# A decoder layer with 32 experts on one core: weights in rows of 8 KB, two tiles for the halves' sums, and later one-hot rows at the last expert

## The chip, the core and the metric

The kernel runs on one core of a Trainium2 chip. The core has TensorE (PE, whose weight loads the profile shows as PEld), VectorE (DVE), ScalarE (ACT), GpSimd (POOL), SyncE (SP, which here issues nearly all transfers) and 16 DMA engines. The metric is the time of one execution on the device in microseconds; less is better.

## What is computed

A decoder layer for 256 tokens of width 1024, all in float32: a projection, two kinds of attention, an output projection, a LayerNorm, and then a mixture of 32 experts of which each token uses four. The experts' part is what the change is about. Cut to that:

```
def moe_ffn(h, w_router, b_router, w1, b1, w2, b2):
    logits = (h @ w_router + b_router)
    top_vals, top_idx = lax.top_k(logits, 4)
    gates = jax.nn.softmax(top_vals, axis=-1)
    ...
    def expert_block(xb, e):                  # tokens of expert e
        act = clamped_swiglu(xb @ w1[e] + b1[e])   # w1[e]: 1024 x 2048, w2[e]: 1024 x 1024
        return act @ w2[e] + b2[e]
    ...
    # every token: sum of its four experts' rows, weighted by gates

def clamped_swiglu(h):
    glu = jnp.minimum(h[..., 0::2], 7.0)
    lin = jnp.clip(h[..., 1::2], -7.0, 7.0)
    return glu * jax.nn.sigmoid(1.702 * glu) * (lin + 1.0)
```

All 32 experts are evaluated, so all weights, 32 x 12.6 MB, pass through the core once.

## The kernel before, in words

The attention comes first (to about 146 us), then a Python loop unrolls the experts e = 0 to 31.

**Weights.** An expert has twelve blocks of 1 MB. Eight are of `w1`: a block holds 256 rows by one half of the columns, so that a partition gets two pieces of 4 KB; blocks 0 to 3 are the first half (n = 0), 4 to 7 the second. Four are of `w2`: 256 whole rows, a partition gets row p and row p + 128, again two pieces of 4 KB. The list `stream` has all 384 blocks in the order in which they are wanted, but for the last four, which are `w2` of the last expert cut by columns, in pieces of 2 KB. There are 23 places of 8 KB a partition (`place`; fifteen in the tile `arena`, eight tiles `later`), and block i goes into the place of block i - 23. `load(n)` writes the transfers up to block n into SP's program; SP works in order, and each transfer waits until the block that had its place has been read. Where they are written: for the experts 0 to 3, 30 and 31 (those that are not `inline`) behind every second step of the first product; for the others in one go, twelve behind the first step of the next expert, since a branch for experts with more than 64 tokens (`more`, taken if the count of expert e - 1 asks for it) stands there and reads the blocks again.

**One expert.** Up to 64 tokens of an expert stand in `XG`. For each half n of the columns PE first writes the bias into `ph[:, n, :]` (`first_biases`), and then makes eight steps k over the rows of `w1`; a step is a product of 64 rows of tokens with two pieces of 512 columns, which lie in the upper and the lower half of the array. Then DVE and ACT make the activation from `ph[:, n, :]` (`swiglu`). At step five of the second half `turn_act` transposes the first half's activation with PE into `ph[:, 0, :]`, and ACT copies it out. `second` makes the second product in eight steps into a bank of its own, with the transposes of the other half behind its third. At even e four matmuls (`combine`) add the pair before to the sums `acc`; at every fourth e (3, 7, ... 27; seven times) `Group` collects the tokens of the next four experts: four runs of eight matmul records into the halves of `ph` in turn, each followed by a copy by ACT and DVE into `XG`.

**The tile `ph`.** It is one tile of two banks of PSUM, `ph[:, 0, :]` and `ph[:, 1, :]`. The framework sets the waits between engines by tiles.

**The last expert.** Ahead of it stands a large branch (label `late`) for counts over the room, not taken here. At the third step of its first half (`at == (0, 2)`) DVE makes the one-hot rows with the gates (`rows_of_last`), PE transposes them, and at the next two steps PE adds expert 30's rows (`combine_first`). `expect` puts a hint for a branch behind an engine's last instruction.

Every engine's program stands in the order in which the Python calls it (`Ordered`); the line of nearly all instructions in the profile is the one helper's, L125.

Of the kernel before, what the change touches and what calls it, by code (L numbers as in the profile page):

```python
# [47 lines left out]
def decoder_layer(ctx, tc, x, w_in, b_in, sinks, w_out, b_out, ln1_g, ln1_b, w_router, b_router,  # L48
# [32 lines left out]
    ph = pmem.tile([P, 2, 512], F32, name="ph")  # L81
# [249 lines left out]
    def scores(n):  # L331
# [4 lines left out]
        for j in range(2):  # L336
            hd = slice(j * HD, (j + 1) * HD)
            pe.matmul(ph[:, j, 0:P], q[hd, 0:P], k[hd, 0:P], start=True, stop=True)
        for j in range(2):
            hd = slice(j * HD, (j + 1) * HD)  # L340
            pe.matmul(ph[:, j, P:P + S], q[hd, P:S], k[hd, :], start=True, stop=True)
        for j in range(2):
            s = ph[:, j, :384].rearrange("p (a b) -> p a b", a=3)
# [76 lines left out]
    for e in range(NE):  # L420
        stream += [w1[0, e, k * 256:(k + 1) * 256, n * FF:(n + 1) * FF].rearrange("(k p) f -> p k f", p=P)
                   for n in range(2) for k in range(4)]
        stream += [w2[0, e, k * 256:(k + 1) * 256, :].rearrange("(k p) f -> p k f", p=P)
                   for k in range(4)]

    again = stream[-4:]
    wl = w2[0, NE - 1].rearrange("(m a i p) f -> m p a i f", a=2, m=2, p=P)
# [211 lines left out]
    aside = (ph[:, 0, :], banks[0])  # L639
# [100 lines left out]
    first = Group(0, (banks[2], banks[3], ph[:, 1, :], banks[1]))  # L740
# [40 lines left out]
    first_biases(ph[:, 0, :], 0, 0)  # L781
# [37 lines left out]
    def turn_act(aT, n, lin, pa=None, i0=0):  # L819

        pa = (TP() if pa is None else pa).rearrange("p (a b) -> p a b", a=4)
        for i in range(i0, i0 + n):
            pe.transpose(pa[:, i, :], V(lin + i * P, P), ident)
# [54 lines left out]
    def last_second(w2s, aT):  # L878
# [14 lines left out]
        turn_act(aT, 2, LIN, ph[:, 0, :], 2)  # L893
# [13 lines left out]
    def over_first(e, b, w1v, xg, lin):  # L907
# [4 lines left out]
        for n in range(wq // 512):  # L912
# [3 lines left out]
            for k in range(KD):  # L916
                for j in range(nq):
                    c0 = j * wq + n * 512
                    pe.matmul(po[j * w:(j + 1) * w, :], xg[:, k, :w],
                              w1v[c0 // FF * 4 + k // 2][:, k % 2, c0 % FF:c0 % FF + 512],  # L920
# [151 lines left out]
    for e in range(NE):  # L1072
# [14 lines left out]
        for n in range(2):  # L1087
            if e or n:
                first_biases(ph[:, n, :], e, n)
            for k in range(KD):  # L1090
                for j in range(2):
                    pe.matmul(ph[j * 64:(j + 1) * 64, n, :], XG[:, k, q * SLOTS:(q + 1) * SLOTS],
                              w1s[n * 4 + k // 2][:, k % 2, j * 512:(j + 1) * 512],
                              start=False, stop=(k == KD - 1))
                at = (n, k)
                if not inline(e) and k % 2:
                    load(e * NW + n * 4 + k // 2 + 1 + NB)
# [24 lines left out]
                if at == (1, 5):  # L1122
                    turn_act(aT, 2, LIN, ph[:, 0, :])
# [131 lines left out]
```

## Time and profile before

| | |
|---|---|
| time, median of 3 runs | 1167.29 us (1166.46 to 1169.7) |
| profiled execution, its own time | 1167.2 us |
| span of that execution | 1165.5 us |
| PE, PEld busy | 1035.2 us (89%), 415.1 us (36%) |
| DVE, ACT busy | 280.4 us (24%), 170.2 us (15%) |
| moved by the DMA engines | 425.79 MB, 365 GB/s over the span |
| packets | 120160, of them under 8 KB 119968 |
| mean granted clock of TensorE | 0.985 |

The page gives busy time by engine and, in 40 slices of the span, shares in tenths and GB/s. A second view sums chosen stretches; a third lists who waited for whom; a fourth, the timeline, lists instructions in order of time, equal ones merged, with the idle time ahead of them and what ended it in brackets. Ends of matmuls are modelled: a run that follows another without a wait starts a little before the other's end. One matmul of float32 leaves two records, and some records are missing, so counts in rows can be a few short.

### The profile page before, as it was taken

To read this page: it belongs to the slowest core of one execution; us is meant where nothing else is said; L and a number is where in the kernel's file an instruction comes from. 1 tells how busy PE (TensorE), PEld (TensorE's weight loads), DVE (VectorE), ACT (ScalarE), POOL (GpSimd) and SP (SyncE) were. 2 spreads that over 40 slices of the span, in tenths; PEclk is the share of its full clock that TensorE was granted. 3 is DMA by queue.
4 is the path that set the end of the run, shared out by engine and by line. 5 is a ranking of instruction groups with operands and counts; after the bars stand their busy time and mean duration, and the time that the engine had idled before them with its cause. 6 is when DMAs were issued, how large, how long until landed. Compare 5 with 4: busy or idle time off the path is not lost. (4 is left out here: it accounts for less than half of the span.)

```text
span 1165.5 us, 11836 instructions
## 1 busy us (share of the span) xinstructions
PE 1035.2 (89%) x4538; PEld 415.1 (36%) x4538; DVE 280.4 (24%) x763; ACT 170.2 (15%) x384; POOL 7.1 (1%) x20
## 2 busy tenths in 40 slices
PE   8789899989899899988899798979998999879985
PEld 7565433333233333332333333333333333333321
DVE  6666521121111111221122111211112111211114
ACT  5433411010100100010000100010101000100101
POOL 0000000000000000000000000000000000000001
PEclk9899999999999999999999999999999999999988
DMA  9987799994769999999999999999999999999992
GB/s 332 263 305 298 269 340 409 409 409 168 296 237 410 359 399 369 401 409 367 409 359 410 395 386 408 409 409 409 409 409 409 409 408 408 409 408 408 408 390 95
DMA packets 120160, 425.79 MB, mean 365 GB/s; under 512 B 8416, under 2 KB 16384, under 8 KB 119968
## 3 DMA queue, kind: packets, MB, share of 16 engines
q1 hardware_dynamic: 118624, 423.07, 93.4%
q10 hardware_dynamic: 1440, 1.41, 0.4%
q8 instruction: 64, 1.05, 0.4%
q14 instruction: 32, 0.26, 0.1%
HBM read 423.40 MB, written 1.05 MB: 364 GB/s over the span
## 5 line engine op out<-in xcount | busy, mean ns | idle before, releaser
L125 PE MATMUL ph<-arena 128*64 128x512 f32 (+3 forms) x1416 | 338.8, 586 | 19.3 <-ACT arena L125 9.0
L125 PE MATMUL bank<-arena 128*64 128x512 f32 (+6 forms) x984 | 268.8, 583 | 6.9 <-DVE arena L125 4.7
L125 PE MATMUL ph<-later,arena 128*64 128x512 f32 x712 | 177.8, 605 | 16.0 <-PEq L968 9.4
L125 PEld LDWEIGHTS ph<-arena 128*64 128x64 f32 (+2 forms) x1416 | 110.6, 140 | 194.7 <-issue 172.3
L125 DVE TENSOR_SCALAR arena<-ph 128x256 f32<-128x256 f32 x128 | 48.3, 419 | 473.6 <-PE ph L125 372.2
L125 PEld LDWEIGHTS bank<-arena 128*64 128x64 f32 (+3 forms) x984 | 87.6, 147 | 157.2 <-issue 140.0
L125 PE MATMUL bank<-later,arena 128*64 128x512 f32 (+1 forms) x432 | 101.0, 606 | 0.9 <-DMA later<-in_w_dram 0.9
L125 PEld LDWEIGHTS ph<-later,arena 128*64 128x64 f32 x712 | 57.8, 139 | 109.3 <-issue 94.7
L125 ACT COPY arena<-bank 128x256 f32<-128x256 f32 (+4 forms) x97 | 43.9, 470 | 314.2 <-DVE arena L125 203.3
L125 PE MATMUL ph<-arena,x_sb 128*128 128x256 f32 x232 | 58.0, 392 | 25.9 <-DVE arena L125 25.9
L125 DVE COPY arena<-bank 64x512 f32<-64x512 f32 (+2 forms) x41 | 27.0, 657 | 224.2 <-PE bank L125 224.2
L125 ACT ACTIVATE arena<-arena 128x256 f32<-128x256 f32 x65 | 27.1, 416 | 297.3 <-DVE arena L125 288.1
L125 PE MATMUL bank<-early,early 128*128 128x512 f32 (+1 forms) x240 | 58.4, 398 | 5.1 <-ACT early L125 5.1
L125 ACT COPY arena<-ph 128x256 f32<-128x256 f32 (+1 forms) x65 | 24.1, 370 | 251.8 <-PE ph L125 251.8
L125 PEld LDWEIGHTS ph<-arena,x_sb 128*128 128x128 f32 x232 | 41.7, 189 | 44.5 <-DVE arena L125 34.4
L125 PE MATMUL ph<-b_s,sel 96*64 96x512 bf16 x128 | 25.4, 386 | 29.1 <-DVE arena L125 29.1
L125 PEld LDWEIGHTS bank<-early,early 128*128 128x128 f32 x240 | 43.9, 206 | 15.2 <-ACT early L125 5.3
L125 DVE TENSOR_TENSOR arena<-arena 128x256 f32<-128x256 f32 (+4 forms) x101 | 45.8, 469 | 7.5 <-DVE arena L125 0.5
L125 PEld LDWEIGHTS bank<-later,arena 128*64 128x64 f32 (+1 forms) x432 | 28.0, 134 | 54.1 <-issue 48.6
L125 DVE TENSOR_SCALAR arena<-ph,cols 128x256 f32<-128x256 f32 x29 | 15.8, 543 | 90.6 <-ACT arena L125 90.6
L125 PE MATMUL bank<-ident,arena 128*128 128x128 f32 x147 | 24.4, 289 | 11.6 <-DVE arena L125 10.0
L125 PEld LDWEIGHTS <-sel 96*64 96x64 bf16 (+1 forms) x132 | 10.8, 108 | 65.6 <-issue 65.4
(105 smaller groups left out, 335.8 us busy)
## 6 DMA issues: line engine op xcount, KB each, us to landing
arena<-in_w_dram SPq DMA_DIRECT2D x244, 1024.0 KB, 18.3
later<-in_w_dram SPq DMA_DIRECT2D x136, 1024.0 KB, 18.4
arena<-in_w_in_dram SPq DMA_DIRECT2D x10, 512.0 KB, 10.7
arena<-in_w_dram SPq DMA_DIRECT2D x8, 512.0 KB, 14.1
arena<-in_w_in_dram SPq DMA_DIRECT2D x3, 1024.0 KB, 9.7
arena<-in_w_out_dram SPq DMA_DIRECT2D x4, 512.0 KB
arena<-in_w_out_dram SPq DMA_DIRECT2D x2, 1024.0 KB
arena<-in_xt_dram SPq DMA_DIRECT2D x4, 256.0 KB, 3.9
```

Of the source, the lines that this page charges most:

```text
L125: ins = getattr(self.engine, name)(*a, **k)
```

## The change

- `w1` comes in blocks of 128 whole rows: a partition gets one row of 8 KB. The columns are still computed by halves, so each of the eight blocks is now read by step k of the first half and again by step k of the second.
- `w2` comes with two neighbouring rows in a partition, again 8 KB in one piece. Row and activation must agree, so `turn_act` now transposes every second column of a stretch of 256. The last four blocks stay cut into pieces of 2 KB.
- For the experts that are not inline, the transfers stand behind each step of the second half instead of every second step of both.
- `ph` becomes two tiles of one bank each.
- The hint for the inline branches stands behind the first step of the second product instead of behind the second pair of transposes; the hints of DVE and ACT for the branch `late` are left out, PE's stays.
- At the last expert `rows_of_last` moves to the second step of the second half, and `combine_first` to the third and fourth.

```
-    ph = pmem.tile([P, 2, 512], F32, name="ph")
+    ph = [pmem.tile([P, 512], F32, name=f"ph{i}") for i in range(2)]
...
-        stream += [w1[0, e, k * 256:(k + 1) * 256, n * FF:(n + 1) * FF].rearrange("(k p) f -> p k f", p=P)
-                   for n in range(2) for k in range(4)]
-        stream += [w2[0, e, k * 256:(k + 1) * 256, :].rearrange("(k p) f -> p k f", p=P)
+        stream += [w1[0, e, k * P:(k + 1) * P, :] for k in range(KD)]
+        stream += [w2[0, e, k * 256:(k + 1) * 256, :].rearrange("(p k) f -> p k f", p=P)
                    for k in range(4)]
...
-    wl = w2[0, NE - 1].rearrange("(m a i p) f -> m p a i f", a=2, m=2, p=P)
+    wl = w2[0, NE - 1].rearrange("(m a p i) f -> m p a i f", a=2, m=2, p=P)
...
-            pe.transpose(pa[:, i, :], V(lin + i * P, P), ident)
+            pe.transpose(pa[:, i, :], V(lin + i // 2 * 2 * P, 2 * P)[:, i % 2::2], ident)
...
-                    pe.matmul(ph[j * 64:(j + 1) * 64, n, :], XG[:, k, q * SLOTS:(q + 1) * SLOTS],
-                              w1s[n * 4 + k // 2][:, k % 2, j * 512:(j + 1) * 512],
+                    pe.matmul(ph[n][j * 64:(j + 1) * 64, :], XG[:, k, q * SLOTS:(q + 1) * SLOTS],
+                              w1s[k][:, n * FF + j * 512:n * FF + (j + 1) * 512],
...
-                if not inline(e) and k % 2:
-                    load(e * NW + n * 4 + k // 2 + 1 + NB)
+                if not inline(e) and n:
+                    load(e * NW + k + 1 + NB)
...
-                if at == (0, 2) and odd:
+                if at == ((0, 2) if e < NE - 1 else (1, 1)) and odd:
                     rows_of_pair(e - 1) if e < NE - 1 else rows_of_last()
-                if e == NE - 1 and at in ((0, 3), (0, 4)):
-                    combine_first(k - 3)
+                if e == NE - 1 and at in ((1, 2), (1, 3)):
+                    combine_first(k - 2)
...
-                    nxt = Group(e + 1, [ph[:, r % 2 ^ 1, :] for r in range(4)])
+                    nxt = Group(e + 1, [ph[r % 2 ^ 1] for r in range(4)])
...
-        second(py, w2s, aT, range(3), odd)
-        turn_act(aT, 2, LIN, ph[:, 0, :], 2)
-        label = f"second{e}" if inline(e) else "late" if e == NE - 2 else None
-        if label:
-            expect(label)
-        if label == "late":
-            expect(label, dve)
-            expect(label, act)
+        second(py, w2s, aT, range(1), odd)
+        if inline(e) or e == NE - 2:
+            expect(f"second{e}" if inline(e) else "late")
+        second(py, w2s, aT, range(1, 3), odd)
+        turn_act(aT, 2, LIN, ph[0], 2)
         second(py, w2s, aT, range(3, 4), odd)
```

How PE's program reads at two places. The first is expert 3, from the last step of its first half on. `ph` is the tile of the sums, `b_s,sel` are a bias matmul's operands, `arena` holds tokens and weights, `ident` marks a transpose; in brackets are the semaphores that a row waits for (DMAHW: a transfer's landing). Before, around the second half's bias:

```order
L125 MATMUL ph<-arena 64x512 [waits DMAHW4_49]
L125 MATMUL ph<-arena 64x512 x3
L125 LDWEIGHTS sel_67
L125 MATMUL ph<-b_s,sel_67 64x512 [waits DVE_49]
L125 LDWEIGHTS sel_67
L125 MATMUL ph<-b_s,sel_67 64x512
L125 MATMUL ph<-arena 64x512 [waits DMAHW5_49]
L125 MATMUL ph<-arena 64x512 x3
```

and before, around the transposes in the same half:

```order
L125 MATMUL ph<-arena 64x512 [waits DMAHW7_49]
L125 MATMUL ph<-arena 64x512 x3
L125 MATMUL ph<-ident,arena 128x128 [waits DVE_49]
L125 MATMUL ph<-ident,arena 128x128
L125 MATMUL ph<-arena 64x512 [waits DMAHW0_49,Activation_49]
L125 MATMUL ph<-arena 64x512 x3
```

After, the same stretch in whole (`ph_95` and `ph_96` are the two tiles):

```order
L125 MATMUL ph_95<-arena 64x512 [waits DMAHW0_49]
L125 MATMUL ph_95<-arena 64x512
L125 LDWEIGHTS sel_67
L125 MATMUL ph_96<-b_s,sel_67 64x512
L125 LDWEIGHTS sel_67
L125 MATMUL ph_96<-b_s,sel_67 64x512
L125 MATMUL ph_96<-arena 64x512 x12
L125 MATMUL ph_95<-ident,arena 128x128 [waits DVE_49]
L125 MATMUL ph_95<-ident,arena 128x128
L125 MATMUL ph_96<-arena 64x512 x4
L125 MATMUL bank_94<-arena 64x512 [waits DMAHW1_49,Activation_49]
```

The second half has lost its waits for landings, for DVE at the bias and for ACT behind the transposes; the first half waits for a landing at each step instead of each second.

The second place is the collecting of the next group's tokens at the same expert. `x_sb` holds the tokens; four rows of matmuls make one run. Before:

```order
L125 MATMUL ph<-arena,x_sb 128x256 [waits Activation_49]
L125 MATMUL ph<-arena,x_sb 128x256 x3
L125 MATMUL ph<-arena,x_sb 128x256 [waits DVE_49]
L125 MATMUL ph<-arena,x_sb 128x256 x3
L125 MATMUL ph<-arena,x_sb 128x256 [waits DVE_49]
L125 MATMUL ph<-arena,x_sb 128x256 x3
```

After:

```order
L125 MATMUL ph_96<-arena,x_sb 128x256 x4
L125 MATMUL ph_95<-arena,x_sb 128x256 [waits Activation_49]
L125 MATMUL ph_95<-arena,x_sb 128x256 x3
L125 MATMUL ph_96<-arena,x_sb 128x256 [waits DVE_49]
L125 MATMUL ph_96<-arena,x_sb 128x256 x3
L125 MATMUL ph_95<-arena,x_sb 128x256 [waits DVE_49]
L125 MATMUL ph_95<-arena,x_sb 128x256 x3
```

The runs took turns between the halves of one tile before; they now take turns between two tiles, and a wait for DVE is one for the copy out of the same tile two runs back.

## Rows read from the trace of the kernel before

**Rows 1.** The page's head, and GB/s in 40 slices of 29.1 us.

```profile
span 1165.5 us, 11836 instructions
GB/s 332 263 305 298 269 340 409 409 409 168 296 237 410 359 399 369 401 409 367 409 359 410 395 386 408 409 409 409 409 409 409 409 408 408 409 408 408 408 390 95
```

**Rows 2.** Stretches: length, busy us by engine (instructions), PE's clock, DMA share, GB/s.

```profile
340.00:680.00 340.00, 305.72 (x1291) 114.18 (x1290) 63.90 (x170) 33.14 (x76) 0.00 (x0) 0.99 0.99 386
680.00:1120.00 440.00, 397.12 (x1682) 144.01 (x1680) 72.96 (x191) 42.45 (x98) 0.00 (x0) 1.00 1.03 409
```

**Rows 3.** Waits: engine and line waited for whom: us in total, times, longest.

```profile
PE ph L125 <- DVE arena L125: 55.6, 55, 1.2
...
PE ph L125 <- ACT arena L125: 15.0, 33, 0.5
...
PEld bank L125 <- DMA later<-in_w_dram: 4.3, 7, 1.5
PEld ph L125 <- DMA arena<-in_w_dram: 3.8, 9, 1.4
```

**Rows 4.** Timeline of PE, experts 21 to 25: start, us, operation, count, [idle before].

```profile
811.76 3.65 PE L125 MATMUL bank<-arena 128*64 128x512 f32 x16
815.25 0.39 PE L125 MATMUL ph<-b_s,sel 96*64 96x512 bf16 x2
...
825.34 0.41 PE L125 MATMUL ph<-b_s,sel 96*64 96x512 bf16 x2 [0.91 <-DVE arena L125]
825.55 5.34 PE L125 MATMUL ph<-arena 128*64 128x512 f32 x24
830.83 0.44 PE L125 MATMUL ph<-ident,arena 128*128 128x128 f32 x2
831.73 1.94 PE L125 MATMUL ph<-later,arena 128*64 128x512 f32 x8 [0.46 <-ACT arena L125]
...
895.09 1.99 PE L125 MATMUL ph<-arena,x_sb 128*128 128x256 f32 x8 [1.24 <-DVE arena L125]
...
935.62 0.39 PE L125 MATMUL ph<-b_s,sel 96*64 96x512 bf16 x2
```

**Rows 5.** Timeline of SP: issues of blocks 23, 71 and 83 (counted from 0).

```profile
147.77 0.38 SPq L143 DMA_DIRECT2D arena<-in_w_dram  x1
...
296.13 0.37 SPq L143 DMA_DIRECT2D later<-in_w_dram  x1
...
340.22 0.37 SPq L143 DMA_DIRECT2D arena<-in_w_dram  x1
```

**Rows 6.** Stretches with packets of nearly one size: 1, 2, 4, 6, 8 KB.

```profile
32.20:36.80 4.60, 4.05 (x23) 3.01 (x24) 2.33 (x6) 0.65 (x2) 0.00 (x0) 1.00 1.10 350
16.50:20.50 4.00, 4.00 (x19) 3.34 (x18) 3.61 (x10) 1.68 (x3) 0.00 (x0) 1.00 1.05 387
210.00:250.00 40.00, 37.17 (x162) 13.17 (x158) 8.11 (x26) 4.53 (x11) 0.00 (x0) 1.00 1.03 409
21.50:23.00 1.50, 1.50 (x8) 1.27 (x7) 1.50 (x4) 0.81 (x2) 0.00 (x0) 1.00 1.03 416
55.20:59.00 3.80, 2.60 (x18) 1.92 (x17) 2.75 (x15) 1.75 (x8) 0.00 (x0) 0.93 0.85 209
```

**Rows 7.** The last expert: timeline of DVE and PE, and one stretch.

```profile
1122.22 1.11 DVE L125 TENSOR_SCALAR arena<-iota,rank,gates 128x128 f32<-128x128 f32 x4 [6.47 <-PEq L1076]
...
1122.71 1.15 PE L125 MATMUL bank<-ident,arena 128*128 128x128 f32 x4 [4.90 <-DVE arena L125]
...
1123.50:1127.50 4.00, 4.00 (x10) 0.87 (x9) 0.00 (x0) 0.65 (x2) 0.00 (x0) 0.50 1.03 387
...
1133.42 0.41 PE L125 MATMUL ph<-b_s,sel 96*64 96x512 bf16 x2 [0.92 <-DVE arena L125]
```

**Rows 8.** DMA issues: operation, count, KB each, median us from issue to landing.

```profile
arena<-in_xt_dram SPq DMA_DIRECT2D x4, 256.0 KB, 3.9
...
out_dram<-arena SPq DMA_DIRECT2D x2, 256.0 KB, 2.0
```

More of the change, by code (lines that the diff above doesn't have):

```diff
@@ L337, in scores @@
             hd = slice(j * HD, (j + 1) * HD)
-            pe.matmul(ph[:, j, 0:P], q[hd, 0:P], k[hd, 0:P], start=True, stop=True)
+            pe.matmul(ph[j][:, 0:P], q[hd, 0:P], k[hd, 0:P], start=True, stop=True)
         for j in range(2):
             hd = slice(j * HD, (j + 1) * HD)
-            pe.matmul(ph[:, j, P:P + S], q[hd, P:S], k[hd, :], start=True, stop=True)
+            pe.matmul(ph[j][:, P:P + S], q[hd, P:S], k[hd, :], start=True, stop=True)
         for j in range(2):
-            s = ph[:, j, :384].rearrange("p (a b) -> p a b", a=3)
+            s = ph[j][:, :384].rearrange("p (a b) -> p a b", a=3)
             for qi, sl, m in QS:
@@ L637, in finish @@
         turn_sums(t, n)
-    aside = (ph[:, 0, :], banks[0])
+    aside = (ph[0], banks[0])
     def add_up(t, n):
@@ L738, in first_biases @@
             first_bias(h[j * 64:(j + 1) * 64, :], e, SLOTS, n * 1024 + j * 512)
-    first = Group(0, (banks[2], banks[3], ph[:, 1, :], banks[1]))
+    first = Group(0, (banks[2], banks[3], ph[1], banks[1]))
     finish(0, 0)
@@ L780, in decoder_layer @@
     norm(1, 1)
-    first_biases(ph[:, 0, :], 0, 0)
+    first_biases(ph[0], 0, 0)
     for r in range(4):
@@ L919, in over_first @@
                     pe.matmul(po[j * w:(j + 1) * w, :], xg[:, k, :w],
-                              w1v[c0 // FF * 4 + k // 2][:, k % 2, c0 % FF:c0 % FF + 512],
+                              w1v[k][:, c0:c0 + 512],
                               start=False, stop=(k == KD - 1))
@@ L1088, in decoder_layer @@
             if e or n:
-                first_biases(ph[:, n, :], e, n)
+                first_biases(ph[n], e, n)
             for k in range(KD):
                 for j in range(2):
-                    pe.matmul(ph[j * 64:(j + 1) * 64, n, :], XG[:, k, q * SLOTS:(q + 1) * SLOTS],
-                              w1s[n * 4 + k // 2][:, k % 2, j * 512:(j + 1) * 512],
+                    pe.matmul(ph[n][j * 64:(j + 1) * 64, :], XG[:, k, q * SLOTS:(q + 1) * SLOTS],
+                              w1s[k][:, n * FF + j * 512:n * FF + (j + 1) * 512],
                               start=False, stop=(k == KD - 1))
                 at = (n, k)
-                if not inline(e) and k % 2:
-                    load(e * NW + n * 4 + k // 2 + 1 + NB)
+                if not inline(e) and n:
+                    load(e * NW + k + 1 + NB)
                 if e == 0 and at == (0, 1):
@@ L1122, in decoder_layer @@
                 if at == (1, 5):
-                    turn_act(aT, 2, LIN, ph[:, 0, :])
-            swiglu(ph[:, n, :], 256, GLU + n * 256, LIN + n * 256, AT + n * 256)
+                    turn_act(aT, 2, LIN, ph[0])
+            swiglu(ph[n], 256, GLU + n * 256, LIN + n * 256, AT + n * 256)
         w2s = wt[e * NW + KD:(e + 1) * NW]
@@ L1129, in decoder_layer @@
         py = banks[4 + odd]
-        second(py, w2s, aT, range(3), odd)
-        turn_act(aT, 2, LIN, ph[:, 0, :], 2)
-        label = f"second{e}" if inline(e) else "late" if e == NE - 2 else None
-        if label:
-            expect(label)
-        if label == "late":
-            expect(label, dve)
-            expect(label, act)
+        second(py, w2s, aT, range(1), odd)
+        if inline(e) or e == NE - 2:
+            expect(f"second{e}" if inline(e) else "late")
+        second(py, w2s, aT, range(1, 3), odd)
+        turn_act(aT, 2, LIN, ph[0], 2)
         second(py, w2s, aT, range(3, 4), odd)
```

## Prediction

> **What bounds the kernel now.** I read the page first, then the stretches, then the waits, then PE's timeline. The span is 1165.5 us [rows 1] and the profiled execution took 1167.2, so 1.7 us lie around the span; the median is 1167.29, so a sum made against 1167.2 stands for it. The reader is to see two regimes in the row of GB/s: it dips up to about the 24th slice (168, 237, 359) and then stays at 408 or 409 to the end. The stretches say the same: 386 GB/s from 340 to 680 us, 409 from 680 to 1120 [rows 2]. That looks like a kernel bound by its transfers. The waits say otherwise [rows 3]: weight loads of PE waited for weights for 4.3 and 3.8 us in the whole run, while PE waited 55.6 us for DVE and 15.0 for ACT, all of it before writes to `ph`. Four experts in a row, from one first bias to the fourth next, take 935.62 - 815.25 = 120.4 us [rows 4], 30.1 each; twelve blocks of 1.0486 MB at 409 GB/s take 12 x 2.564 = 30.8. So PE sets the pace, the transfers run level with it, and the 23 places take up the rest. An edit that helps one of the two alone gains little; this change touches both.
>
> **Part one: two tiles.** Before, the first bias matmul of the second half waits for DVE, although DVE reads the other half of `ph`; in the order after, that wait is gone, as is ACT's wait behind the two transposes. The first shows 0.91 us of idle time [rows 4]. A run that waits for nothing starts before the modelled end of the one ahead (811.76 + 3.65 = 815.41, the next at 815.25), so the loss is 0.91 + 0.16 = 1.07. The second shows 0.46, and with 0.07 of such overlap 0.53. Together 1.60 an expert. In a group's rows three of four runs wait 1.24 us for the copy of the run ahead (one stands in [rows 4]); after, run r waits for the copy of run r-2, which has a whole run of 1.99 us to finish in, so 3 x (1.24 + 0.07) = 3.93 go in each of seven groups. What is late next? The transposes at step five need DVE's product, which has five steps of matmul (5.34 us, [rows 4]) to come; I cost that at nothing. PE's four experts become 120.4 - 4 x 1.60 - 3.93 = 110.1, 27.5 each.
>
> **Part two: rows of 8 KB.** The trace before has stretches in which nearly all packets have one size [rows 6]: rows of 1 KB at 350 GB/s, 2 KB at 387, 4 KB at 409, 6 KB at 416. For one of 16 engines that is 46.8, 84.7 and 160.3 ns for 1, 2 and 4 KB: 75.6 ns for the step from 2 to 4 KB, hence 151 for 4 KB and 9 fixed for a packet. 6 KB should then take 236 ns, 417 GB/s; the row has 416. For 8 KB I get 2 x 160.3 - 9 = 311 ns, 421 GB/s, 2.49 us a block against 2.564. The bounds are 2.564 (no gain) and 2.46 (a little beyond the line); I take 2.49, since 6 KB lies on the line. A row that speaks against it, 8 KB packets at 209 GB/s, is a rival below.
>
> A rule against this part: the Trainium skill ("DMA: Bandwidth & Descriptors", "Where 436 GB/s comes from") has HBM bind loads at some 358 GB/s, so that row length could not matter; the 409 here is already above that, and the trace disagrees. The Trainium skill (same title, section "Why small descriptors are slow (HBM only)") gives three cycles for a packet on a bus of 32 bytes: 131 cycles for 4 KB and 259 for 8 KB, 1.2% in place of the 2.9% worked out above; by that estimate the sum would be some 13 us later. The steps from 1 to 6 KB here show 9 ns, more than it gives, and I go by them.
>
> **Part three: eight blocks in the first half, later releases.** Each block now serves both halves. For the first four experts places come free in the second half alone. The first reload, at 147.77 [rows 5], moves behind seven more steps of 0.86, a bias and the small work between: 6.6 us later, 154.4. For experts 4 to 29 all twelve places come free behind the next expert's first step, as before. Does the transfer queue run dry while PE waits for the eighth block? When that block lands, four blocks of this expert and eleven of the next are still to come: 15 x 2.49 = 37 us. Up to the next release PE has one step, a half (7), the second product with its transposes (8), a combination (3.5: four matmuls of 0.86) or a group's rows (8), at most 26 us, and 31 if five more are lost to a slow clock. So it does not, and the period is that of the transfers, 12 x 2.49 = 29.9, over PE's 27.5.
>
> **Part four: the rest.** Transposes read every second column: 0.22 us each [rows 4], four an expert. Between no cost and double, that is 0 to 0.9 us; PE has 2.4 to spare, so only the last expert could show it. The hint for the branch stands two steps earlier on PE, again where PE has slack. At the last expert DVE now comes out of the big branch 6.47 us after its last work [rows 7], and PE idles 4.90 for its one-hot rows; after, these rows are wanted seven steps and a bias, 6.2 us, later, and the first half of that expert is stretched by its eight landings (20 us), so even a jump twice as long without its hint is hidden. That gain is PE's alone and not in the sum.
>
> **The sum.** Up to the fifth expert's overflow PE gains 5 x 1.60 + 3.93 = 11.9 us. The block loaded at 296.13 [rows 5] is issued 11.9 earlier, and 0.9 more since one step frees it: 283.3. By then the 48 blocks from 154.4 on (120 us, to some 275) have landed, so the later start in part three costs nothing; its cover is 8 us. The twelve blocks from 283.3 are through at about 314, and the next release, 340.22 before, comes at 340.22 - 11.9 - 1.6 = 326.7. From there the queue is never dry. To the last block of the last expert's first matrix it carries 297 blocks, 297 x 2.49 = 739.5 us, and 1.05 MB of norm rows at the 1 KB rate, 3.0. Issue and landing take 2.4 beside it: a 256 KB store lands in 2.0 us, a like load in 3.9, 0.6 to 0.75 of them transfer [rows 8], which bounds it by 1.4 and 3.2. It lands at 1071.6. Then follow one step (0.9) and what stands in the trace from 1133.42 [rows 7] to 1165.5, 32.1, less ACT's 0.53, plus the moved transposes (1.15, [rows 7]; 1.1 with the overlap) and combination (1.7, two steps' worth): 34.4. PE's clock may be down behind the waits: after the 4.90 before, the granted clock was 0.50 from 1123.5 to 1127.5 [rows 7], 1.2 GHz of 2.4, and four such us lose two; I put 2 for 0 to 4. 1071.6 + 0.9 + 34.4 + 2 = 1108.9, and with 1.7 around the span **1110.6 us**.
>
> **Rivals.** *Row length changes nothing* (packets are cut to 4 KB, or something other than the packet sets 409). For it: four sizes in short stretches are no steady state. Then 297 x 0.074 = 22 us more, 1132.6; a part of the gain lies between. *Long rows are slower*, the case on the other side: the nearest row with 8 KB packets shows 209 GB/s [rows 6]. Each added 0.01 us a block costs 3 us, so the change loses from 2.68 us a block, 391 GB/s, on, and at 300 GB/s it would stand near 1410. Against it: those loads fill 32 partitions each, the weights 128. *PE stays the bound*: it waits in each first half, its clock falls, and it needs over 29.9 an expert; at 31 the last expert starts at 326.7 + 25 x 31 = 1102, and the end is 1102 + 7 + 34.4 + 3.7 = 1147. Against it: a PE that is late no longer waits, so the cause removes itself. Faster than forecast by more than the bounds would need blocks under 2.46; PE alone, 77 us shorter, would end near 1080.
>
> **How the numbers follow.** Forecast with its bounds (1098 to 1120): 0.60. Row length of little or no use (1120 to 1137): 0.21. PE bound (1137 to 1164): 0.07. Under 1098: 0.04. Long rows slower, past 1171: 0.06; about even: 0.02. The range 1098 to 1137 holds 0.81. What a measurement of this kernel can tell from no change is about 0.3%, 3.5 us: faster 0.92, same 0.02, slower 0.06.
>
> **What would show it.** In the profile after: no wait of PE for DVE at the second half's bias and the four runs of a group without gaps; PE waiting for weights in the first halves instead, far above 8 us in total; some 420 GB/s in place of 409 from 340 us to the end, with no dip; packets of 8 KB. A steady 409 makes the first rival true, a rate under 391 the second; dips at each expert with PE busy, the third.

## The result, and the profile after

The changed kernel takes 1130.04 us (median of 4, 1127.85 to 1131.67) and the kernel before 1166.88 in the same comparison: a ratio of 0.9681, interval 0.9654 to 0.9709. The forecast was 1110.6 with a range of 1098 to 1137. So the sign is right and the time lies in the range, but 36.8 us came where 56.7 were forecast, and the forecast's own bounds, 1098 to 1120, are missed: 1130 falls into the part of the range that was set aside for "row length of little or no use". The profiled execution of after took 1131.67 us, 1.7 of them around the span.

The head of its page, with GB/s in 40 slices of 28.3 us, answers to [rows 1]:

```profile
span 1130.0 us, 11863 instructions
...
GB/s 331 264 298 322 239 244 421 422 420 342 371 247 421 420 420 365 423 421 371 418 403 420 382 422 421 421 419 420 420 420 420 421 419 421 421 421 420 405 325 73
```

Where the queue is full it now moves 419 to 423 GB/s, as forecast (421). But the row is not without dips from 340 us on, as the forecast wanted it: 365, 371, 403, 382, and 405 ahead of the tail. The stretches that answer to [rows 2], and then the dips one by one (length, busy us by engine with instructions, TensorE's clock, DMA share, GB/s):

```profile
340.00:680.00 340.00, 322.79 (x1356) 123.74 (x1354) 67.29 (x179) 35.19 (x81) 0.00 (x0) 0.98 0.99 407
680.00:1080.00 400.00, 369.89 (x1538) 134.29 (x1536) 67.38 (x177) 38.72 (x89) 0.00 (x0) 0.97 1.00 414
...
440.00:452.00 12.00, 12.00 (x56) 5.95 (x53) 3.17 (x9) 0.79 (x2) 0.00 (x0) 1.00 0.77 289
510.00:520.00 10.00, 10.00 (x49) 3.83 (x46) 3.13 (x8) 0.42 (x1) 0.00 (x0) 1.00 0.72 273
565.00:580.00 15.00, 13.69 (x62) 4.93 (x60) 3.13 (x8) 0.79 (x2) 0.00 (x0) 1.00 1.00 384
637.00:647.00 10.00, 10.00 (x46) 4.05 (x42) 3.13 (x8) 0.79 (x2) 0.00 (x0) 1.00 0.85 318
647.00:1065.00 418.00, 387.75 (x1620) 140.51 (x1618) 72.33 (x190) 41.15 (x95) 0.00 (x0) 0.98 1.01 420
1065.00:1082.00 17.00, 17.00 (x69) 5.77 (x66) 2.29 (x5) 1.73 (x4) 0.00 (x0) 1.00 0.69 266
```

Against 420 GB/s the four short stretches lose 12 x (1 - 289/420) = 3.7, and in the same way 3.5, 1.3 and 2.4 us, 10.9 together; the one from 1065 to 1082 loses 6.2. The four lie where experts 10, 12, 14 and 16 fetch their norm rows, the last where SP meets its conditional branch. From 647 to 1065 nothing is lost.

The waits, which answer to [rows 3], have changed sides. TensorE's 55.6 us for VectorE ahead of `ph` are gone from the list, and of the 15.0 for ScalarE 0.3 are left; it waits for weights instead (PEld is its weight loads):

```profile
PEld ph L125 <- DMA arena<-in_w_dram: 50.2, 36, 2.3
...
PEld ph L125 <- DMA later<-in_w_dram: 17.5, 10, 3.3
```

TensorE's timeline in one expert answers to [rows 4]. The second half's bias (818.63) follows without a wait, the transposes and the products behind them too, and the waits stand in the first half, ended by one block each (811.90, then 814.39, which is left out here, then 816.88: 2.49 us apart):

```profile
811.90 1.08 PE L125 MATMUL ph<-arena 128*64 128x512 f32 x4 [1.19 <-DMA arena<-in_w_dram]
...
816.88 1.97 PE L125 MATMUL ph<-arena 128*64 128x512 f32 x4 [0.51 <-DMA arena<-in_w_dram]
818.63 0.64 PE L125 MATMUL ph<-b_s,sel 96*64 96x512 bf16 x2
```

SP's issues of blocks 23, 71 and 83 answer to [rows 5]. The first two stand at 155.80 and 284.33, for a forecast of 154.4 and 283.3; the third was forecast for 326.7:

```profile
326.03 0.33 SPq L143 DMA_DIRECT2D arena<-in_w_dram  x1
```

And the last expert, which answers to [rows 7]: the last w1 block ends TensorE's wait at 1092.62, VectorE takes up the first half at once, and the transposes for the one-hot rows stand at 1097.27, with no wait that the row names.

```profile
1092.62 1.08 PE L125 MATMUL ph<-later,arena 128*64 128x512 f32 x4 [2.38 <-DMA later<-in_w_dram]
1093.53 0.46 PE L125 MATMUL ph<-b_s,sel 96*64 96x512 bf16 x2
1093.82 0.76 DVE L125 TENSOR_SCALAR arena<-ph 128x256 f32<-128x256 f32 x2 [12.42 <-PE ph L125]
...
1097.27 0.66 PE L125 MATMUL bank<-ident,arena 128*128 128x128 f32 x4
```

So the forecast's chain stands, with one link stretched: the last w1 block, forecast for 1071.6, ends TensorE's wait 21.0 us later, and the span ends at 1130.0 where 1108.9 was forecast, 21.1 later. Two waits of SP are candidates for what stretched it. One view lists whom SP waited for:

```profile
SPq L143 <- DMA arena<-in_ln_g_dram: 56.2, 4, 15.1
...
SPq L1075 <- SPq L1075: 19.3, 6, 5.1
```

The first is a weight load that waits for a norm row. In the order of instructions every DMA of SP and of ScalarE uses the next of eight completion semaphores, DMAHW0 to DMAHW7, and waits until that one's last user has landed. A norm row issued by ScalarE takes a turn among them, so the weight load that comes to its semaphore next can't be issued until the norm row is there, and no load behind it either. Two delays add up in such a wait. At the first dip SP has stood since 429.5 when ScalarE, which waits for VectorE itself, issues the norm row at 436.34; then the row, of 128 KB, takes some 8 us to land beside the blocks under way. SP goes on at 444.57, after 15.1 us. From 430 to 450 us the busy share of the DMA engines, in slices of 0.5 us and in tenths, shows that the queue had run empty by then, and was not merely slow (the second row: count, KB, median us from issue to landing):

```profile
DMA  9899898999989999999898998844200948999937
...
arena<-in_ln_g_dram ACTq DMA_DIRECT2D x1, 128.0 KB, 8.2
...
436.34 0.39 ACTq L125 DMA_DIRECT2D arena<-in_ln_g_dram  x1
...
444.57 0.33 SPq L143 DMA_DIRECT2D arena<-in_w_dram  x1
```

The second is the branch to the late overflow. In SP's order before, it stood behind all loads; in the changed kernel the scheduler put it ahead of the last four w1 blocks, the eight pieces of the last w2 and two norm rows:

```
before:  451  L143 DMA later<-in_w_dram 128x2x1024     (last w1 block)
         459  L149 DMA arena<-in_w_dram 128x2x512      (last w2 piece)
         461  L169 DMA arena<-in_ln_b_dram 128x1024
         463  L1076 COMPARE_AND_BRANCH
after:   449  L143 DMA later<-in_w_dram 128x2048       (w1 block 375 of 379)
         450  L1075 COMPARE_AND_BRANCH
```

The rows of that branch on SP are the comparison at 1058.8 and nine semaphore waits behind it (columns: ns least, median, most; first and last start):

```profile
L1075 SPq EVENT_SEMAPHORE  x9: 17/17/17, 1064.0 to 1078.4; - x9
...
L1075 SPq COMPARE_BRANCH  x1: 53/53/53, 1058.8 to 1058.8; - x1
```

For 20 us SP waits until the transfers under way have landed, one after the other, and issues none; then the queue is empty.

### The profile page after: what moved, and what is told of

The parts are those of the page before. It is cut to its first block, busy times and chain, and to the rows that moved or that the text cites. A ratio compares the mean times of both kernels' runs of the same rounds, so it can differ in the third digit from the quotient of the medians.

```text
span 1130.0 us, 11863 instructions
## 1 busy us (share of the span) xinstructions
PE 1044.0 (92%) x4538; PEld 424.2 (38%) x4538; DVE 280.5 (25%) x763; ACT 170.4 (15%) x384; POOL 7.1 (1%) x20
## 5 line engine op out<-in xcount | busy, mean ns | idle before, releaser
L125 PE MATMUL ph<-arena 128*64 128x512 f32 (+3 forms) x1416 | 364.8, 603 | 33.9 <-DMA arena<-in_w_dram 24.3
L125 PE MATMUL bank<-arena 128*64 128x512 f32 (+6 forms) x984 | 264.1, 579 | 5.9 <-DVE arena L125 4.0
L125 PE MATMUL ph<-later,arena 128*64 128x512 f32 x712 | 188.7, 607 | 19.4 <-DMA later<-in_w_dram 9.5
L125 PE MATMUL bank<-later,arena 128*64 128x512 f32 (+1 forms) x432 | 96.6, 597 | 0.0
L125 PE MATMUL ph<-arena,x_sb 128*128 128x256 f32 x232 | 52.4, 382 | 0.0
L125 PEld LDWEIGHTS ph<-ident,arena 128*128 128x128 f32 x128 | 20.3, 207 | 52.1 <-DVE arena L125 27.0
L125 PE MATMUL ph<-ident,arena 128*128 128x128 f32 x128 | 32.4, 335 | 0.1
L125 DVE SCALAR_TENSOR_TENSOR arena<-arena 128x256 f32<-128x256 f32 (+1 forms) x75 | 31.4, 419 | 3.7 <-DMA arena<-in_ln_b_dram 1.1
```

The costliest lines, as they stand in the source:

```text
L125: ins = getattr(self.engine, name)(*a, **k)
```

## The experiments

All ratios are to the kernel before, run beside each (its medians: 1168.39 us beside e1 to e4, 1169.8 beside e5 to e8, 1168.65 beside e9 to e12). The two right columns are of one profiled execution each; equal kernels differ there by 6 us (first two rows).

| run | us, median (range) | ratio (95%) | last w1 block ends TensorE's wait | span's end |
|---|---|---|---|---|
| changed kernel | 1130.04 (1127.85 to 1131.67) | 0.9681 (0.9654 to 0.9709) | 1092.6 | 1130.0 |
| e9, the same again | 1128.43 (1125.22 to 1130.89) | 0.9657 (0.9633 to 0.9680) | 1086.5 | 1123.5 |
| e1 two tiles alone | 1138.07 (1137.14 to 1139.45) | 0.9737 (0.9697 to 0.9777) | | 1135.8 |
| e2 all but two tiles | 1158.97 (1156.42 to 1160.7) | 0.9922 (0.9893 to 0.9952) | | 1154.7 |
| e3 loads ahead of branch | 1130.66 (1123.47 to 1133.29) | 0.9662 (0.9605 to 0.9718) | 1085.7 | 1127.2 |
| e4 norm rows by GpSimd | 1126.03 (1124.88 to 1128.37) | 0.9638 (0.9597 to 0.9679) | 1085.4 | 1122.8 |
| e5 both | 1121.53 (1118.88 to 1125.13) | 0.9585 (0.9549 to 0.9621) | 1080.5 | 1120.5 |
| e6 w2 in 4 KB rows | 1131.57 (1129.51 to 1136.4) | 0.9673 (0.9635 to 0.9710) | 1096.3 | 1134.3 |
| e7 one-hot rows early | 1126.96 (1122.98 to 1131.02) | 0.9632 (0.9592 to 0.9671) | | 1125.4 |
| e8 two hints back | 1129.53 (1126.85 to 1130.97) | 0.9650 (0.9616 to 0.9685) | 1089.6 | 1128.3 |
| e10 both, rows early | 1123.47 (1122.12 to 1125.04) | 0.9612 (0.9590 to 0.9634) | | 1122.1 |
| e11 both, w2 in 4 KB rows | 1128.14 (1126.92 to 1129.65) | 0.9650 (0.9628 to 0.9672) | 1086.3 | 1127.5 |
| e12 two tiles, norm rows by GpSimd | 1136.21 (1135.37 to 1137.46) | 0.9719 (0.9697 to 0.9741) | | 1135.3 |

### e1: two tiles and nothing else

```
-    ph = pmem.tile([P, 2, 512], F32, name="ph")
+    ph = [pmem.tile([P, 512], F32, name=f"ph{i}") for i in range(2)]
     (and ph[:, n, :] becomes ph[n] throughout)
```

> The kernel before, with the halves' sums in two tiles of PSUM and nothing else changed; weight rows stay 4 KB and SP's loads stand where they stood. Theory (TensorE's waits for the two halves were the bound, and the transfers are next in line): TensorE catches up with the transfers, and the end is set by 297 blocks of 2.564 us from block 83's issue at 340.2, plus about 11 us that the queue loses around the four pairs of norm rows, plus a tail of 37: 1146 to 1157 us. Rival (two tiles carry the whole gain, the 8 KB rows are for nothing): 1128 to 1133. Rival (rows carry it, tiles nothing): 1164 to 1168.

1138.07 us: none of the three. The waits of TensorE for VectorE and ScalarE ahead of `ph` are gone as in the changed kernel, block 83 is issued at 325.04, and the queue runs at its old rate nearly without a dip, 408 GB/s from 680 to 1080 us and, before that, in the stretch that shows 386 in [rows 2]:

```profile
340.00:680.00 340.00, 319.60 (x1360) 119.16 (x1358) 67.02 (x179) 35.16 (x81) 0.00 (x0) 1.00 1.02 405
```

The expectation started from 340.2, where block 83 stands before, and forgot that the faster TensorE brings this forward by 15.2 us by itself (the forecast had 13.5 for the same thing). And the norm rows cost less here than the 11 us that it put down: SP waited 28.5 us for them in all, not 56.2, with rates of 365 and 382 GB/s at the worst two. So two tiles alone give 30.3 us of the 37 that the whole change gives.

### e2: all of the change but the two tiles

```
-    ph = [pmem.tile([P, 512], F32, name=f"ph{i}") for i in range(2)]
+    ph_all = pmem.tile([P, 2, 512], F32, name="ph")
+    ph = [ph_all[:, i, :] for i in range(2)]
```

> The changed kernel with the halves' sums in one tile again; rows of 8 KB, their later issue, the strided transposes and the late one-hot rows stay. Theory: TensorE waits for VectorE and ScalarE at the halves as in the kernel before, its period sets the pace from about block 83 on, and faster transfers only wait; the strided transposes add 0.2 to 0.4 us an expert: 1158 to 1172 us. Rival (long rows carry the gain): 1128 to 1140.

1158.97 us, as the theory had it. TensorE's two waits are back to the tenth (the code is a line longer, so L126):

```profile
PE ph L126 <- DVE arena L126: 55.6, 55, 1.2
...
PE ph L126 <- ACT arena L126: 15.0, 33, 0.5
...
PE bank L126 <- DVE arena L126: 10.9, 10, 2.0
```

All but the tiles gains 9.4 us with this TensorE. Not all of that is the rows' doing: the 4.90 us that TensorE stood for the last expert's one-hot rows before [rows 7] are gone with their later place, as the last row shows beside its counterpart in the kernel before:

```profile
PE bank L125 <- DVE arena L125: 15.5, 10, 4.9
```

What long rows alone give with one tile, no run shows. The two parts are nearly additive: 30.3 + 9.4 = 39.7, and both together give 37.3 (0.9681 of 1168.39).

### e3: SP's transfers ahead of its branch

```
 def column_chunk:
-            sync.dma_start(out=dst[:, a], in_=src[:, a])
+            last[sync] = sync.dma_start(out=dst[:, a], in_=src[:, a])
 def count:
-            for eng in (pe, act, dve):
+            for eng in (pe, act, dve, sync):
 ahead of the late branch:
-            last.clear()
+            for eng in (pe, act, dve):
+                last.pop(eng, None)
```

The late branch's count is read on SP behind its last weight load; the order is then that of the kernel before, norm rows included.

> The changed kernel, with SP's last 14 transfers (4 w1 blocks, 8 pieces of w2, 2 norm rows) put ahead of its conditional branch, as in the kernel before; nothing else. Theory (at that branch SP stands until all transfers under way have landed, and the queue runs dry for 6 to 9 us): the last w1 block lands 6 to 9 us sooner, 1120 to 1125 us. Rival (the end is set by TensorE, or by a rate that the memory as a whole gives, so a gap only moves): 1128 to 1132.

The dip at the branch is gone; the dips at the norm rows stand:

```profile
440.00:455.00 15.00, 13.64 (x62) 5.12 (x61) 3.13 (x8) 0.79 (x2) 0.00 (x0) 1.00 0.84 307
...
1065.00:1080.00 15.00, 15.00 (x64) 5.16 (x62) 2.29 (x5) 1.37 (x3) 0.00 (x0) 1.00 1.01 419
```

The last w1 block lands at 1085.7, 6.9 us sooner than in the first profile of the changed kernel but only 0.8 sooner than in the second (e9). Most of the 6.9 isn't the edit's: this execution lost 6.0 us at the norm rows, reckoned as above, and that one 10.9. Some 2 us are left for a dip of 6.2; e5 shows what takes the place of the rest.

And the time is 1130.66, the rival's. More is given back in the tail, on three engines:

```profile
1085.73 1.52 PE L125 MATMUL ph<-later,arena 128*64 128x512 f32 x4 [1.45 <-DMA later<-in_w_dram]
...
1087.46 2.98 PE L125 MATMUL ph<-arena 128*64 128x512 f32 x8
...
1090.64 0.76 DVE L125 TENSOR_SCALAR arena<-ph 128x256 f32<-128x256 f32 x2 [12.56 <-PEq L1076]
...
1092.80 1.15 PE L125 MATMUL bank<-ident,arena 128*128 128x128 f32 x4 [2.36 <-DVE arena L125]
```

TensorE is through with the first half at 1087.0, but VectorE takes it up at 1090.64, only when the next half's run of eight matmul records has ended too (1087.46 + 2.98 = 1090.44); in the changed kernel it did so 0.3 us after the second half's bias had begun. The one-hot rows stand behind that work on VectorE, and TensorE waits 2.36 us for them. From the landing to the end this kernel takes 41.5 us for the changed kernel's 37.4, and VectorE's delay of over 3 us is the larger part of it. The view of the branch shows where it comes from: TensorE's own part of it has moved too.

```profile
L1076 PEldq EVENT_SEMAPHORE  x2: 51/51/51, 1090.5 to 1090.6; - x2
...
L1076 PEldq COMPARE_BRANCH  x1: 374/374/374, 1086.2 to 1086.2; - x1
```

Here TensorE compares at 1086.2, when the first half is done, and sets the branch's semaphores at 1090.6, behind the first matmuls of the second half; VectorE's wait ends with them (`PEq L1076`). In the changed kernel TensorE is past its branch at 1082.8, ten us before the last w1 block. So the scheduler moved that branch when SP's order was changed, and the edit isn't the pure reordering of SP that it was meant to be. Nor do the times decide much here, with this kernel's runs 10 us apart: the dip is shown to go, its worth in time is not shown by this run.

### e4: norm rows issued by GpSimd

```
 def fetch_rows:
-            act.dma_start(out=ROWS[:, i, :], in_=src[0:1, q * 256:(q + 1) * 256].to_broadcast([P, S]))
+            pool.dma_start(out=ROWS[:, i, :], in_=src[0:1, q * 256:(q + 1) * 256].to_broadcast([P, S]))
```

> The changed kernel, with the four pairs of small norm-row loads (experts 10, 12, 14, 16) issued by GpSimd instead of ScalarE, so that they no longer share the eight completion semaphores that SP's weight loads take in turn. Theory (SP waits for a small load's landing to have its semaphore back, and the queue loses 1.4 to 3.7 us at each pair, 10.8 in all): 1117 to 1122 us. Rival (the gaps belong to buffers that TensorE frees late at these experts, or to the small loads' own transfer): 1128 to 1132.

All four dips are gone (415 GB/s below; the other three stretches have 419, 419 and 420), with the same rows of the same size fetched at the same experts; the dip at the branch stays:

```profile
440.00:452.00 12.00, 11.73 (x52) 3.81 (x48) 2.92 (x8) 0.79 (x2) 0.55 (x1) 1.00 1.02 415
...
1055.00:1075.00 20.00, 19.60 (x82) 6.57 (x80) 2.29 (x5) 1.74 (x4) 0.00 (x0) 1.00 0.68 265
```

So neither late buffers nor the small transfers themselves made the gaps: the shared semaphores did. GpSimd cuts its transfers into fewer packets, 87 for ScalarE's 288 from 430 to 450 us, so two things changed; but its rows still take 7.1 and 5.8 us to land there, the queue doesn't notice, and SP's list of waits has no norm rows any more. Of the 10.9 us, 7.2 reach the last landing (1085.4 for 1092.6; the 1084.9 in the expectation of e5 is the end of TensorE's run before that landing), but against e9's profile, with its shallower dips, only 1.1 do; the branch loses 7.4 in place of 6.2. The time, 1126.03, lies between theory and rival; by its interval alone it can't be told from the changed kernel.

### e5: both edits

The diffs of e3 and e4 together.

> The two edits of the runs before together: SP's last 14 transfers ahead of its branch, and the norm rows issued by GpSimd. In their traces the first saved 6.9 us of landing time of the last w1 block (1085.7 for 1092.6) and the second 7.7 (1084.9). Theory (the two losses are separate and both lie on the transfers, which set the end): the last w1 block lands at 1076 to 1079, the tail is 38 to 41.5 us, so 1115 to 1121 us, some 11 us below the changed kernel. Rival (one of them gives back what the other gains, or another engine is next): 1124 to 1130.

1121.53 us, half a us above the theory's range and clear of the changed kernel (the interval 0.9549 to 0.9621 touches neither 0.9654 to 0.9709 nor e9's 0.9633 to 0.9680). This is the lowest median of the study, though e10 can't be told from it. Its queue is full from 327 us to the last expert:

```profile
327.00:1067.00 740.00, 700.06 (x2942) 261.39 (x2938) 136.23 (x360) 74.69 (x172) 4.50 (x8) 0.98 1.01 419
1067.00:1080.00 13.00, 10.27 (x47) 2.95 (x46) 0.68 (x1) 0.58 (x1) 0.00 (x0) 1.00 0.91 355
```

From 1067 on the rate falls, though SP has issued everything in time. The DMA view of 1067 to 1080 shows why:

```profile
DMA packets 1223, 4.62 MB, mean 355 GB/s; under 512 B 94, under 2 KB 94, under 8 KB 849
```

849 - 94 = 755 packets are of the last w2's pieces, which have rows of 2 KB and are queued behind the last w1 blocks. The 16 DMA engines don't wait for each other: some are at these pieces while others still have rows of the w1 blocks. Before the last w1 block is whole, 755 x 2 KB = 1.5 MB of w2 have been moved, 3.7 us at 420 GB/s. The tail has e3's late VectorE as well, with TensorE's semaphores of the branch set at 1085.1 and 1085.2:

```profile
1085.20 0.76 DVE L125 TENSOR_SCALAR arena<-ph 128x256 f32<-128x256 f32 x2 [13.87 <-PEq L1076]
```

### e6 and e11: w2 in rows of 4 KB, contiguous transposes

```
-        stream += [... rearrange("(p k) f -> p k f", p=P)      (w2)
+        stream += [... rearrange("(k p) f -> p k f", p=P)
-    wl = w2[0, NE - 1].rearrange("(m a p i) f -> m p a i f", a=2, m=2, p=P)
+    wl = w2[0, NE - 1].rearrange("(m a i p) f -> m p a i f", a=2, m=2, p=P)
-            pe.transpose(pa[:, i, :], V(lin + i // 2 * 2 * P, 2 * P)[:, i % 2::2], ident)
+            pe.transpose(pa[:, i, :], V(lin + i * P, P), ident)
```

> The changed kernel with w2 in rows of 4 KB as before and its transposes contiguous again; w1 keeps its rows of 8 KB. Theory (transfers set the end, the strided transposes lie beside them): 99 of the 297 blocks take 2.564 for 2.494 us each, 7 us later, 1135 to 1139 us. Rival (strided transposes, 207 for 140 ns a weight load and 335 for 300 ns a product, 128 of each, lie on the path): 13 us come back, 7 are paid, 1122 to 1126 us. Rival (slack at the norm rows and at the branch takes up the difference): 1128 to 1132.

> The kernel of both edits, with w2 in rows of 4 KB and its transposes contiguous again. With the gaps closed there is no slack left to take up slower rows. Theory (99 blocks by 2.564 for 2.494 us): 7 us more than both edits, 1126 to 1130 us. Rival (the rate goes by more than the row, as the 416 GB/s with mixed rows says, 2.521 us for each of 297 blocks): 8 us more, not told apart from the theory; rival (strided transposes lie on the path as well and are worth as much): 1119 to 1123 us.

On the changed kernel (e6) nothing can be told apart: 1131.57 us. On the kernel of both edits (e11) the 6.6 us forecast as 7 are there: 1128.14 for 1121.53. The last w1 block lands 5.8 us later than in e5. So a third of the rows is worth about its 7 us where the queue has no gaps, and the transposes, which change in the same run, nothing that shows beside it, though they do cost. That gaps swallow the 7 us in e6 is argued: its four stretches at the norm rows lose 2.8 us against its own 416 GB/s, less than in any profile of the changed kernel, but no run tests it. The groups of the transposes in the page (busy us, mean ns), first of the changed kernel, then of e6:

```profile
L125 PEld LDWEIGHTS ph<-ident,arena 128*128 128x128 f32 x128 | 20.3, 207 | 52.1 <-DVE arena L125 27.0
L125 PE MATMUL ph<-ident,arena 128*128 128x128 f32 x128 | 32.4, 335 | 0.1
```

```profile
L125 PEld LDWEIGHTS ph<-ident,arena 128*128 128x128 f32 x128 | 12.8, 140 | 52.1 <-DVE arena L125 26.2
L125 PE MATMUL ph<-ident,arena 128*128 128x128 f32 x128 | 28.0, 300 | 0.1
```

With w1 in rows of 8 KB and w2 in rows of 4 KB the queue of e11 moves 416 GB/s, between the two rates:

```profile
340.00:1065.00 725.00, 679.69 (x2846) 248.25 (x2844) 133.06 (x352) 73.16 (x168) 4.52 (x8) 0.97 1.02 416
```

### e7 and e8: one-hot rows early, hints back

```
e7: -                if at == ((0, 2) if e < NE - 1 else (1, 1)) and odd:
    +                if at == (0, 2) and odd:
    -                if e == NE - 1 and at in ((1, 2), (1, 3)):
    -                    combine_first(k - 2)
    +                if e == NE - 1 and at in ((0, 3), (0, 4)):
    +                    combine_first(k - 3)
e8: +        if e == NE - 2:
    +            expect("late", dve)
    +            expect("late", act)
```

> The changed kernel with the last expert's one-hot rows made after the third block of the first half, and their products one and two blocks later, as in the kernel before. Theory (VectorE comes back from its branch some 6 us after it left, while TensorE waits for the last w1 blocks anyway until 1092.6): the stall at the transposes is inside that wait, 1128 to 1132 us, no difference to be measured. Rival (the late place is worth what VectorE's return cost before, 4.9 us): 1133 to 1137 us.

> The changed kernel with the two prefetch hints of VectorE and ScalarE at the late branch put back. Theory (both engines have 6 us to come back while TensorE waits for blocks, hints or not): 1128 to 1132 us, and the jump on VectorE takes 5 to 6 us as in the kernel before. Rival (hints shorten the way back, or their fetches cost something elsewhere): a difference of over 3 us either way.

1126.96 and 1129.53 us beside 1128.43 for the unedited kernel (e9): no difference that can be told. That fits the forecast, which had both small parts hidden behind the last blocks' landings.

### e9: the changed kernel again

> The changed kernel itself, unedited, beside the three other runs of this call: 1128 to 1132 us, as measured. Differences of a few us between the edits are read against this run.

1128.43 us. Its profiled execution is 6.4 us shorter than the first one, and the same dips are there with other depths:

```profile
440.00:452.00 12.00, 10.59 (x47) 3.48 (x44) 3.13 (x8) 0.79 (x2) 0.00 (x0) 1.00 0.80 308
```

With 385, 402 and 419 GB/s in the other three stretches they lose 3.2, 0.8, 0.6 and 0.0 us here, 4.6 in place of 10.9: 6.3 us less, near the 6.5 by which the two spans differ. The gaps are not a fixed cost, then, and the 10.9 of the first profile is the largest sum seen; e3, e7 and e8, which keep ScalarE's rows, have 6.0, 7.3 and 6.1. The dip at the branch is steadier: 280 GB/s from 1060 to 1078 us, 6.0 us, for 6.2.

### e10: both edits, rows early

The diffs of e5 and e7 together.

> The kernel of both edits (loads ahead of SP's branch, norm rows by GpSimd), with the last expert's one-hot rows at their earlier place of the kernel before. In the trace of both edits TensorE stood 2.7 us ahead of the last expert's transposes, since VectorE took up the first half's sums only at 1085.2, 2.3 us after TensorE had left them. Theory (early rows do not stand behind these sums, so this wait goes, and VectorE's way back from the branch falls into the wait for blocks): 2 to 4 us less than both edits, 1117 to 1120 us. Rival (VectorE's return of 6 us is exposed instead, as in the kernel before): 1121 to 1126 us.

1123.47 us: the theory falls. VectorE's late pick-up is gone, but now its way back from the branch is exposed, as in [rows 7]:

```profile
1079.92 1.11 DVE L125 TENSOR_SCALAR arena<-iota,rank,gates 128x128 f32<-128x128 f32 x4 [5.92 <-ACTq L1076]
...
1080.42 1.16 PE L125 MATMUL bank<-ident,arena 128*128 128x128 f32 x4 [4.35 <-DVE arena L125]
```

One wait of 2.4 us is exchanged for one of 4.35. Whether the late place (e5) is better stays within the intervals.

### e12: two tiles, old rows, norm rows by GpSimd

e1 with e4's edit.

> The kernel before with two tiles for the halves' sums and the norm rows issued by GpSimd; rows of 4 KB throughout, its loads stand ahead of the branch as they did. Beside the kernel of both edits (1121.5) it gives what long rows are worth where the queue is never dry. Theory (297 blocks by 2.564 for 2.494 us, 21 us, less the 6 us by which 4 KB rows could leave earlier at the first reload): 1134 to 1140 us. Rival (two tiles with both edits give it all): 1120 to 1125 us.

1136.21 us. Beside e5, in which the queue is as full, long rows with all that comes with them are worth 14.7 us, inside the theory, where rows alone were reckoned at 21; beside e10, which ran next to it and makes the one-hot rows early as this kernel does, 12.7. Some of the rest is the price of the layout: with the old one TensorE needs only four w1 blocks in the last expert's first half. There it begins the second half 31.5 us before the span's end, at 1103.84 of 1135.3:

```profile
1103.84 0.39 PE L125 MATMUL ph<-b_s,sel 96*64 96x512 bf16 x2
```

In e5 that half begins at 1082.22, 38.3 us before the end, since the one-hot rows, their products and the wait for them stand behind it. That part of the 6 us is read from two timelines, not tested by a run of its own.

## Why the prediction was right, and where it was not

**What bounds the kernel.** Right that TensorE's waits at `ph` bound it, and that the transfers are next: e1 takes the waits away and the queue runs at 405 to 408 GB/s; e2 leaves them and they are 55.6 and 15.0 us again. Wrong was the sentence that an edit that helps one of the two alone gains little. Two tiles alone gave 30.3 us, and the forecast's own first rival said so: 1132.6 with no use of the rows is 34.6 below the kernel before. The transfers were level with TensorE only from 680 us on; before that they had lost time to its waits, 386 GB/s in [rows 2] where e1 has 405, and 15.2 us up to block 83.

**Part one** was right. The group's runs and the second half's bias no longer wait, and block 83 moved from 340.22 to 326.03 for a forecast of 326.7.

**Part two** was right: 2.49 us a block, 420 to 422 GB/s against 421, worked out from short stretches [rows 6]. The rival that row length changes nothing falls with e11 and e12, and so does the one that long rows are slower. The Trainium skill ("DMA: Bandwidth & Descriptors", "Where 436 GB/s comes from") says that the HBM side binds loads at some 358 GB/s, and its figure is half of a stack's 716 GB/s, a share for two cores. This kernel runs on one; 419 over 740 us in e5 speaks against it here, and the measurement decides.

**Part three** holds the step that failed: "From there the queue is never dry." Its argument asked whether TensorE frees places in time, and there it held: no gap from 647 to 1065. What it left out are waits of the engine that issues. The term 297 x 2.49 + 3.0 + 2.4 = 744.9 us, from block 83 to the last w1 block, measured 1092.6 - 326.0 = 766.6 in the profiled run, 21.7 too many. Of these, 10.9 are the norm rows' semaphores (e4 takes all four dips away), 6.2 SP's branch (e3 takes that dip away), 2.0 the block at 420 GB/s, 2.497 us for 2.49; 2.6 stay unassigned. The second profile (e9) has the same terms with another size: 1086.5 - 326.3 = 760.2, 15.3 too many, of which the same three take 4.6, 6.0 and 2.0. Both waits were to be seen before the run: in the trace before SP waits for norm rows as well,

```profile
SPq L143 <- DMA arena<-in_ln_g_dram: 58.1, 4, 15.5
```

which cost little while TensorE was the bound (its waits for weights there are single microseconds, [rows 3]), and the branch's new place stands in the order of the changed kernel's SP rows. The forecast looked at TensorE's order alone.

With both gone (e5) the term is 1080.5 - 326.5 = 754.0, 9.1 more than forecast. Here 2.0 are again the 2.497, 3.7 the w2 pieces moved in between, and 13 x (1 - 355/420) = 2.0 their lower rate; 1.4 stay open. So of the 17.1 us of dips in the first profile 12.6 come back in the term, and of the 10.6 in e9's 6.2: with SP's loads ahead of its branch, the w2 pieces take part of what the branch took. The forecast had counted the last w1 block as alone at the end of the queue.

**Part four** was right in size and sign: the transposes cost 67 ns a weight load and 35 a product and nothing that the times show (e6, e11); early rows and hints make no difference that can be told on the changed kernel (e7, e8). The one-hot rows are hidden only as long as the last blocks come late: in e10 VectorE's return costs 4.35 us again.

**The tail** was forecast as 0.9 + 34.4 + 2 = 37.3 us from the last landing and took 37.4, and 37.0 in e9. The slow clock that it allowed for is there: 0.59 from 1093 to 1097.

```profile
1093.00:1097.00 4.00, 4.00 (x14) 0.99 (x10) 2.63 (x8) 0.42 (x1) 0.00 (x0) 0.59 1.05 401
```

**The rivals.** TensorE as the bound (1147) falls: in the changed kernel it waits for weights, and between the dips the queue is full. The 1130 measured lies beside the 1132.6 of "row length changes nothing", by chance: the rate went up as forecast, and other losses of the same size took its place. The time alone would have confirmed the wrong rival; the slices of GB/s tell them apart. One side remark of the forecast is off: 77 us less than 1167 is 1090, not "near 1080"; nothing rests on it.

## What to carry to other kernels

When an edit makes the transfers the bound, look through everything the issuing queue waits for, not only for whether buffers come free: semaphores that it shares with another engine's small loads, which tie it to that engine's progress as well as to their landing, and branches on that engine, at which it stands until all that is under way has landed. Waits that cost little while a compute engine was the bound turn into gaps then; here they cost 17 of the 57 us forecast in the first profile and 11 in the second, and a one-word edit with an ordering edit brought 7 to 9 us back. And compare the order of the issuing engine's instructions before and after as well: a scheduler moves a branch past the loads without a line of the diff saying so, and an edit made to undo that can move another engine's branch, as in e3. And a landing read from one execution against another is no measure of an edit, where equal kernels lie 6 us apart.

## What was not expected of the hardware

- A 128 KB load issued by ScalarE beside a full queue took 8.2 us to land, against the 3.9 us of a 256 KB load in [rows 8]; issued by GpSimd it took 7.1.
- A block is whole only when the slowest of the DMA engines has done its rows, and the others go on with what is queued behind: in e5, 755 packets of 2 KB overtook rows of w1 in 13 us, at 355 GB/s. The Trainium skill ("DMA: Bandwidth & Descriptors", "Two DMAs through the same engine are not ordered") says that nothing orders DMAs across the 16 engines; the trace agrees, with these packets.
- Reading every second column of float32 as the operand of a transpose took 207 ns a weight load for 140, and 335 ns a product for 300. The Trainium skill ("SBUF — State Buffer", "Door 1: The DMA port swizzle") has a stride of up to four float32 free in SBUF; for what TensorE reads here the rows disagree.
- The depth of the gaps at the norm rows differs between executions of one kernel, 10.9 and 4.6 us, and with it the span, 1130.0 and 1123.5.
